# Heads 4 to 7 of the inverse's 64-level products go to the other 64 PSUM rows, alternating between two column halves of the array

## The chip, the cores and the metric

The kernel runs on one core of one Trainium2 chip. What counts is the device time of a run in microseconds; the median of several runs is given, and one execution was taken with the hardware profiler. Engines are named as in the profile: PE is TensorE's matmul, PEld its weight load, DVE is VectorE, ACT is ScalarE, POOL is GpSimd, SP is the queue from which most DMAs are issued.

## The reference

One layer with a bidirectional gated delta rule (8 heads of 128, two directions), a gated short convolution, a merge and a layer norm over 2048 latent and 256 context tokens. The part that matters here is the inverse of a unit lower triangular matrix in each chunk:

```
m = jnp.where(tri_strict, jnp.einsum('bhncd,bhnsd->bhncs', k_beta, k) * decay, 0.0)
eye = jnp.eye(CHUNK, dtype=jnp.float32)
t_inv = lax.linalg.triangular_solve(eye + m, jnp.broadcast_to(eye, m.shape), left_side=True, lower=True)
u = jnp.einsum('bhncs,bhnsv->bhncv', t_inv, v_beta)
w = jnp.einsum('bhncs,bhnsd->bhncd', t_inv, k_beta * jnp.exp(g_cum)[..., None])
...
def step(s, xs):
    v_new = u_i - jnp.einsum('bhck,bhkv->bhcv', w_i, s)
    o = jnp.einsum('bhck,bhkv->bhcv', q_dec_i, s) + jnp.einsum('bhcs,bhsv->bhcv', qk_i, v_new)
    s = s * d_i[..., None, None] + jnp.einsum('bhck,bhcv->bhkv', k_dec_i, v_new)
```

## The kernel before

The kernel has three stages: the input projections (to about 1890 us of the span), the window, in which the delta rule runs (about 1890 to 2865 us), and the dense tail.

The window makes 36 blocks: 18 chunks of 128 tokens, two directions, forward and backward in turn, so block 14 and every other even one goes forward. Blocks are counted here from 0, in the order of their 64-level products. The loop (`window`) is a pipeline over blocks: in one turn block k+2 gets its matrix N (`gram` "N" on L158 to L163, then `inv_base`), block k has the middle of its inverse done (`inv_w16` to `inv_d64`), and block k-1 is used (`st_ks`, `st_v`, `st_o`, `st_u`). From block 20 on the products behind N and QK were kept in DRAM by the other direction and are loaded (L151), so that those turns have no gram products.

Between these steps stand fillers: 24 to 27 dense 128x512 matmuls a turn (L1244, L1246, L1248, tile pf) of the output branches. PE's order is written out by hand. For the other engines a scheduler picks the order at build time, and each engine then runs its list strictly in that order.

The inverse of one block goes up in levels. The 16-level is done on DVE (L186 to L188, fifteen steps on the tile R16, shown as R and rb), and ACT copies its end into r32 (L191). Then come products on PE at 16, 32 and 64. A 64-level turn is, on PE: `inv_w64` (L273, eight heads, contracting over 64 rows, the result in 64 rows of a PSUM tile pinv), nine fillers, `inv_d64` (L283, again eight heads), the gram products of block k+2 (L158), nine fillers, `st_ks` of the next block (L295). ACT copies the first product into w64 (L276), and writes minus the second into R (L284), on which st_v then works.

A 64-level product before contracts over rows p1 (or p2) and leaves all eight heads in the same 64 PSUM rows, so all eight use the same quarter of the array, one after the other. Each fp32 matmul stands in the trace as two records.

What else the prediction speaks of: `visit_decay` (gcb: the DMA on L104, eight DVE steps L140, the ACT exponential L142, the DVE product L143, into which N and QK are then multiplied on L163); ACT copies gram's PSUM into zat (L161) before DVE reads it on L163; ACT takes four pieces of N (L172) and L175, and DVE goes on with L176; DVE's vh (L297) reads st_ks.

Of the kernel before, what the change touches and what calls it, by code (L numbers as in the profile page):

```python
# [18 lines left out]
H = 8  # L19
# [18 lines left out]
class Kern:  # L38
# [229 lines left out]
    def inv_w64(self, v):  # L268
        nc = self.nc
        (p1, p2), = self.blocks(v["d"], 64)  # L270
        wp = self.pi.tile([P, H, 64], F32, name="pinv")
        for h in range(H):
            nc.tensor.matmul(wp[p2, h, :], v["N"][p1, h, p2], v["r64t"][p1, h, :], start=True, stop=True)  # L273
        v["w64"] = self.g2.tile([P, H, 64], F32, name="w64", bufs=1)
        with self.tc.high_priority(100):
            nc.scalar.copy(out=v["w64"][p2], in_=wp[p2])  # L276

    def inv_d64(self, v):
        nc = self.nc
        (p1, p2), = self.blocks(v["d"], 64)  # L280
        dp = self.pi.tile([P, H, 64], F32, name="pinv")
        for h in range(H):
            nc.tensor.matmul(dp[p1, h, :], v["w64"][p2, h, :], v["r64"][p2, h, :], start=True, stop=True)  # L283
        nc.scalar.mul(out=v["R"][p1, :, p2], in_=dp[p1], mul=-1.0)  # L284


    def st_ks(self, v):
# [1353 lines left out]
```

## Time and profile before

| what | value |
|---|---|
| three runs | 3212.18, 3214.05, 3216.02 us; median 3214.05 us |
| the profiled execution | 3216.19 us |
| its span, first to last instruction | 3214.5 us |
| mean granted TensorE clock over the span | 0.965 |
| PE busy | 2939.6 us, 91% of the span |
| PEld busy | 2410.3 us, 75% |
| DVE busy | 2197.9 us, 68% |
| ACT busy | 1518.0 us, 47% |
| POOL busy | 1405.7 us, 44% |

Busy shares are averages over the three stages; only the window holds the changed products. A busy PE is not a PE at its peak, since a matmul's end is modelled.

### The profile page before, as it was taken

The page shows a single profiled execution, that of the slowest core. Times are in us where ns is not written, and L with a number is a line of the kernel's source. Part 1 is how long each engine was busy: PE and PEld are TensorE (multiplying, and loading weights), DVE is VectorE, ACT ScalarE, POOL GpSimd, SP SyncE. Part 2 cuts the span into 40 slices and gives each one's busy share as a digit, 9 for nine tenths or more (in the row PEclk, how much of TensorE's full clock was granted, in tenths as well). Part 3 has the DMA queues.
Part 4 walks back from the last instruction along what each step waited for, and adds up shares of the span by engine and source line. Part 5 has one row for each costly group of instructions (what it writes and reads, how often), then busy time and mean ns, then how long its engine had stood idle before and what let it go on. Part 6 is the DMA issues. An engine that isn't in the chain of part 4 may idle for free.

```text
span 3214.5 us, 60268 instructions
## 1 busy us (share of the span) xinstructions
PE 2939.6 (91%) x22089; PEld 2410.3 (75%) x22089; DVE 2197.9 (68%) x5663; ACT 1518.0 (47%) x3405; POOL 1405.7 (44%) x1016
## 2 busy tenths in 40 slices
PE   7899889999998999999999978999998888896897
PEld 4678668888887777788878767888887777784776
DVE  7756746566655575565552268888889999867399
ACT  4563553333345746333344335565655666653121
POOL 3543547766567555566666401111111132315264
PEclk9999999999999999999999989999999889998999
DMA  5533763323565433132243377676687777777742
GB/s 212 142 109 86 231 214 121 102 79 113 179 192 173 134 86 100 53 86 85 79 124 109 111 282 253 220 268 222 214 299 257 242 237 267 240 264 251 243 153 102
DMA packets 405381, 557.24 MB, mean 173 GB/s; under 512 B 28244, under 2 KB 278613, under 8 KB 404060
## 3 DMA queue, kind: packets, MB, share of 16 engines
q1 hardware_dynamic: 382158, 520.77, 51.0%
q10 hardware_dynamic: 22926, 32.62, 2.8%
q8 instruction: 173, 2.83, 0.4%
q14 instruction: 124, 1.02, 0.1%
HBM read 391.66 MB, written 161.64 MB: 172 GB/s over the span
## 4 chain that ended last, share of the span: by engine, by line
PE 43%; DVE 27%; DMA 8%; issue 7%; ACT 6%; POOL 5%; SPq 1%; ACTq 0%; DVEq 0%; POOLq 0%
PE pd L758 12%; PE pd L760 12%; PE pd L759 11%; DVE rb L187 3%; DMA gcb<-gcd 3%; POOL al L342 3%; DVE rb L186 2%; DVE gcb L140 2%; DVE R L188 2%; ACT n L172 1%; DVE t L1003 1%; POOL s L744 1%; DVE S L328 1%; DVE gcb L143 1%; DVE t L1005 1%
## 5 line engine op out<-in xcount | busy, mean ns | idle before, releaser
L758 PE MATMUL pd<-bh,ah 128*128 128x512 f32 x2240 | 891.3, 398 | 10.3 <-ACT u L778 5.8
L760 PE MATMUL pd<-bh,al 128*128 128x512 f32 x2240 | 878.7, 392 | 0.0
L759 PE MATMUL pd<-bl,ah 128*128 128x512 f32 x2240 | 878.2, 392 | 0.0
L342 POOL TENSOR_TENSOR al<-s,ah 128x512 fp32r<-128x512 f32 x348 | 478.4, 1378 | 471.2 <-ACT ah L341 466.2
L342 POOL TENSOR_TENSOR al<-raw,ah 128x512 fp32r<-128x512 f32 x260 | 371.9, 1435 | 323.6 <-ACT ah L341 288.9
L758 PEld LDWEIGHTS pd<-bh,ah 128*128 128x128 f32 x2240 | 424.6, 190 | 98.9 <-issue 6.6
L760 PEld LDWEIGHTS pd<-bh,al 128*128 128x128 f32 x2240 | 424.1, 189 | 90.7 <-POOL al L342 0.2
L759 PEld LDWEIGHTS pd<-bl,ah 128*128 128x128 f32 x2240 | 424.8, 190 | 85.9
L341 ACT CAST ah<-s 128x512 fp32r<-128x512 f32 x352 | 214.6, 618 | 298.5 <-PE pd L759 261.7
L341 ACT CAST ah<-raw 128x512 fp32r<-128x512 f32 x264 | 162.3, 616 | 257.8 <-PE pd L759 166.3
L744 DVE TENSOR_TENSOR s<-s,raw 128x512 f32<-128x512 f32 x80 | 107.0, 1338 | 220.7 <-POOL s L744 220.7
L1244 PE MATMUL pf<-ah,wh 128*128 128x512 f32 x512 | 212.4, 416 | 44.4 <-DMA wh<-w_ahd 17.7
L138 POOL TENSOR_TENSOR qd<-qd,qT 128x1024 f32<-128x1024 f32 x32 | 75.7, 2367 | 393.7 <-ACT qd L137 376.7
L1248 PE MATMUL pf<-ah,wl 128*128 128x512 f32 x512 | 218.4, 427 | 2.5 <-DMA wl<-w_ald 2.5
L1246 PE MATMUL pf<-al,wh 128*128 128x512 f32 x512 | 211.0, 412 | 0.7 <-POOL al L342 0.6
L187 DVE TENSOR_TENSOR rb<-rb,n 128x56 f32<-128x56 f32 (+5 forms) x540 | 171.6, 318 | 7.1
L1244 PEld LDWEIGHTS pf<-ah,wh 128*128 128x128 f32 x512 | 101.4, 198 | 66.5 <-issue 29.4
L188 DVE TENSOR_TENSOR R<-R,rb 128x56 f32<-128x56 f32 (+5 forms) x540 | 131.3, 243 | 5.5
L1020 ACT ACTIVATE t<-t 128x512 f32<-128x512 f32 (+1 forms) x112 | 67.2, 600 | 142.2 <-DVE t L1005 142.1
L118 POOL TENSOR_TENSOR kt<-kt,kd 128x1024 f32<-128x1024 f32 x36 | 73.0, 2029 | 137.5 <-DMA kt<-kd 130.8
L315 PE MATMUL pst<-S,qd 128*128 128x128 f32 x512 | 105.5, 288 | 20.3 <-ACT v L307 12.0
L1248 PEld LDWEIGHTS pf<-ah,wl 128*128 128x128 f32 x512 | 100.9, 197 | 26.8 <-DMA wl<-w_ald 6.1
(353 smaller groups left out, 5941.3 us busy)
## 6 DMA issues: line engine op xcount, KB each, us to landing
raw<-in_w_in SPq DMA_DIRECT2D x160, 512.0 KB
kT<-kTd SPq DMA_DIRECT2D x36, 512.0 KB
gcb<-gcd SPq DMA_DIRECT2D x36, 512.0 KB
kt<-kd SPq DMA_DIRECT2D x36, 512.0 KB
vh<-vd SPq DMA_DIRECT2D x36, 512.0 KB
wh<-w_bhd SPq DMA_DIRECT2D x32, 512.0 KB
wl<-w_bld SPq DMA_DIRECT2D x32, 512.0 KB
qT<-qTd SPq DMA_DIRECT2D x32, 512.0 KB
```

The source lines that it names most:

```text
L187: nc.vector.tensor_tensor(out=rbv, in0=rbv, in1=bc(n16[:, :, i:i + 1], w), op=ALU.mult)
L188: nc.vector.tensor_tensor(out=R[:, :, c0:c1], in0=R[:, :, c0:c1], in1=rbv, op=ALU.add)
L315: nc.tensor.matmul(po[:, j, :], v["qd"][:, h, :], S[:, h, :], start=True, stop=False)
L341: self.nc.scalar.copy(out=hi, in_=src)
L342: (eng or self.nc.gpsimd).tensor_tensor(out=lo, in0=src, in1=hi.bitcast(F32), op=ALU.subtract)
L744: eng.tensor_tensor(out=o, in0=a, in1=b, op=op)
L758: mm(ps, hi[:, k, :], bh, start=(first and k == 0), stop=False, skip_group_check=not first)
L759: mm(ps, hi[:, k, :], bl, start=False, stop=False, skip_group_check=not first)
L760: mm(ps, lo[:, k, :], bh, start=False, stop=(last and k == 3), skip_group_check=not first)
L1244: mm(ps, wh[:, k, :], ah, start=(k == 0), stop=False)
L1246: mm(ps, wh[:, k, :], al, start=False, stop=False)
L1248: mm(ps, wl[:, k, :], ah, start=False, stop=(k == KT - 1))
```

## The change

In both products the heads are taken in pairs, h and h + 4. Heads 0 to 3 write the PSUM rows that they wrote before, heads 4 to 7 the other 64 rows, which are the other 64 columns of the array; the rows of the array (the contraction) stay the same. What was one ACT instruction on 64 rows and eight heads becomes two on 64 rows and four heads each, in `inv_w64` and in `inv_d64`.

```diff
         wp = self.pi.tile([P, H, 64], F32, name="pinv")
-        for h in range(H):
+
+        for h in range(4):
             nc.tensor.matmul(wp[p2, h, :], v["N"][p1, h, p2], v["r64t"][p1, h, :], start=True, stop=True)
+            nc.tensor.matmul(wp[p1, h + 4, :], v["N"][p1, h + 4, p2], v["r64t"][p1, h + 4, :], start=True, stop=True)
         v["w64"] = self.g2.tile([P, H, 64], F32, name="w64", bufs=1)
         with self.tc.high_priority(100):
-            nc.scalar.copy(out=v["w64"][p2], in_=wp[p2])
+            nc.scalar.copy(out=v["w64"][p2, 0:4], in_=wp[p2, 0:4])
+            nc.scalar.copy(out=v["w64"][p2, 4:8], in_=wp[p1, 4:8])
...
         dp = self.pi.tile([P, H, 64], F32, name="pinv")
-        for h in range(H):
+        for h in range(4):
             nc.tensor.matmul(dp[p1, h, :], v["w64"][p2, h, :], v["r64"][p2, h, :], start=True, stop=True)
-        nc.scalar.mul(out=v["R"][p1, :, p2], in_=dp[p1], mul=-1.0)
+            nc.tensor.matmul(dp[p2, h + 4, :], v["w64"][p2, h + 4, :], v["r64"][p2, h + 4, :], start=True, stop=True)
+        nc.scalar.mul(out=v["R"][p1, 0:4, p2], in_=dp[p1, 0:4], mul=-1.0)
+        nc.scalar.mul(out=v["R"][p1, 4:8, p2], in_=dp[p2, 4:8], mul=-1.0)
```

The scheduler lays out ACT, DVE, POOL and SP anew, since the number of ACT instructions changed. In the changed kernel the lines behind the edit stand five lower (L158 and L142 are unmoved, L1248 is L1253); the new ones are L274 and L275 for the first product, L278 and L279 for its copies, L286 and L287 for the second product, L288 and L289 for its results.

ACT's list in block 14, before, from the end of the 32-level to the first gram copy:

```order
L260 ACTIVATE r_21466<-pinv 32x8x32
L262 ACTIVATE r64t<-pinv 32x8x32 [waits PE_49]
L266 ACTIVATE R<-r_21466,m64l 128x8x64 [waits Activation_49]
L276 COPY w_21621<-pinv 64x512 [waits PE_49]
L266 ACTIVATE R<-r_21466,m64h 128x8x64
L191 ACTIVATE r_21334<-R_21286,m16l 128x8x16 [waits DVE_49]
L191 ACTIVATE r_21334<-R_21286,m16h 128x8x16
L142 ACTIVATE gcb<-gcb 128x1024
L284 ACTIVATE R<-pinv 64x8x64 [waits PE_49,Activation_49]
L161 COPY zat<-gram 128x512 [waits PE_49]
```

The same place of the changed kernel (r_21362 is block 15's r32, of which R_21314 is the 16-level result on DVE):

```order
L262 ACTIVATE r64t<-pinv 32x8x32 [waits PE_49]
L266 ACTIVATE R<-r_21494,m64l 128x8x64 [waits Activation_49]
L266 ACTIVATE R<-r_21494,m64h 128x8x64
L278 COPY w_21649<-pinv 64x256 [waits PE_49]
L142 ACTIVATE gcb<-gcb 128x1024 [waits DVE_49]
L191 ACTIVATE r_21362<-R_21314,m16l 128x8x16 [waits DVE_49]
L191 ACTIVATE r_21362<-R_21314,m16h 128x8x16
L279 COPY w_21649<-pinv 64x256
L288 ACTIVATE R<-pinv 64x4x64 [waits PE_49,Activation_49]
L289 ACTIVATE R<-pinv 64x4x64
L161 COPY zat<-gram 128x512 [waits PE_49]
```

The one copy of w64 stood ahead of L191 and L142; now its second half stands behind them. So it is in blocks 6, 8, 10, 12, 14, 16, 18 and 26 (L142, then L191 twice, in between), in block 19 (L191 twice, then L142) and in block 4 (L191 twice alone); in block 20 both halves stand behind L191 twice and L142. In the other 25 blocks the two halves follow each other directly, and in the odd blocks 5 to 17 they stand ahead of L191 as the one copy did.

PE's list at the second product of block 14 in the changed kernel, the last filler ahead of it and the gram products behind it (before, the eight L283 had one wait, on the first of them):

```order
L1251 MATMUL pf<-al_15726,wh 128x512
L286 MATMUL pinv<-r_21494,w_21649 64x64 [waits Activation_49]
L287 MATMUL pinv<-r_21494,w_21649 64x64 [waits Activation_49]
L286 MATMUL pinv<-r_21494,w_21649 64x64
L287 MATMUL pinv<-r_21494,w_21649 64x64
...
L158 MATMUL gram<-kT 128x128 [waits DMAHW6_49]
L158 MATMUL gram<-kT 128x128 x7
```

PE's order of steps is the same; the second matmul of the product now waits for the second copy by itself.

## Rows read from the trace of the kernel before

**Rows 1.** The page's first lines: span, and busy time of each engine.
```profile
span 3214.5 us, 60268 instructions
PE 2939.6 (91%) x22089; PEld 2410.3 (75%) x22089; DVE 2197.9 (68%) x5663; ACT 1518.0 (47%) x3405; POOL 1405.7 (44%) x1016
```
**Rows 2.** By stretch: us, then PE, PEld, DVE, ACT, POOL busy; clock, DMA share, GB/s.
```profile
2266.00:2319.20 53.20, 49.79 (x754) 43.76 (x753) 47.04 (x196) 31.88 (x66) 9.00 (x6) 1.00 0.68 219
...
2400.00:2860.00 460.00, 399.36 (x5785) 344.35 (x5784) 415.48 (x1707) 285.77 (x789) 114.85 (x74) 0.93 0.76 255
```
**Rows 3.** Chain that ended last, 2266 to 2296 us, by line.
```profile
by line: DMA gcb<-gcd 29.3%; DVE rb L187 21.4%; DVE rb L186 9.9%; DVE S L328 9.2%; DVE gcb L143 7.9%; DVE R L188 7.5%; DVE gcb L140 5.8%; ACT n L172 5.6%; issue 5.1%; DVE vh L297 5.0%; DVE QK L163 3.8%; DVE N L163 2.3%; DVE gt L1187 2.0%; A
```
**Rows 4.** What DVE waited for, 2000 to 2372 us: total, times, longest.
```profile
DVE n L176 <- ACT n L175: 21.8, 13, 1.7
DVE t L128 <- DMA gcb<-gcd: 12.5, 13, 3.9
```
**Rows 5.** What PE waited for, 1900 to 2860 us: total, times, longest.
```profile
PE pst L295 <- DVE ot L1285: 16.5, 10, 2.8
...
PE pinv L256 <- ACT w32i L245: 8.7, 10, 4.5
PE pinv L205 <- DVE R L188: 8.5, 2, 4.3
```
**Rows 6.** PE in order of time around block 14: start, length, instruction.
```profile
2270.70 1.14 PE L273 MATMUL pinv<-r64t,N 64*64 64x64 f32 x16 [0.39 <-ACT r64t L262]
...
2274.03 1.14 PE L283 MATMUL pinv<-r,w 64*64 64x64 f32 x16
2275.11 2.05 PE L158 MATMUL gram<-kT 128*128 128x128 f32 x16
...
2279.06 2.07 PE L295 MATMUL pst<-S,kT 128*128 128x128 f32 x16
```
**Rows 7.** Chain that ended last: the first and last of its fourteen 64-level products.
```profile
1904.72 1.32 PE pinv L273 x16
...
2860.46 1.09 PE pinv L283 x16
```
**Rows 8.** Busy time of instructions on pinv in two stretches, as in rows 2.
```profile
2743.00:2743.90 0.90, 0.86 (x14) 0.86 (x15) 0.00 (x0) 0.00 (x0) 1.00 0.95 332
2294.40:2294.95 0.55, 0.54 (x48) 0.54 (x48) 0.00 (x0) 0.00 (x0) 1.00 0.90 335
```
**Rows 9.** ACT in order of time around block 14.
```profile
2269.87 0.38 ACT L260 ACTIVATE r<-pinv 32x256 f32<-32x256 f32 x1
...
2271.88 0.58 ACT L276 COPY w<-pinv 64x512 f32<-64x512 f32 x1 [0.48 <-PE pinv L273]
...
2275.62 0.40 ACT L191 ACTIVATE r<-R,m16l 128x128 f32<-128x128 f32 x1 [2.41 <-DVE R L188]
...
2276.22 1.04 ACT L142 ACTIVATE gcb<-gcb 128x1024 f32<-128x1024 f32 x1
2277.29 0.59 ACT L284 ACTIVATE R<-pinv 64x512 f32<-64x512 f32 x1
```
**Rows 10.** DVE in order of time around block 14.
```profile
2275.30 0.28 DVE L188 TENSOR_TENSOR R<-R,rb 128x120 f32<-128x120 f32 x1
...
2277.30 2.37 DVE L143 TENSOR_TENSOR gcb<-gcb,cc 128x1024 f32<-128x1024 f32 x1
...
2280.53 0.67 DVE L163 TENSOR_TENSOR N<-gram,gcb 128x512 f32<-128x512 f32 x1
2281.13 0.59 DVE L297 SCALAR_TENSOR_TENSOR vh<-pst,ngam,vh 128x128 f32<-128x128 f32 x2
2283.39 0.35 DVE L176 SCALAR_TENSOR_TENSOR n<-n,m16h,n 128x128 f32<-128x128 f32 x1 [1.68 <-ACT n L175]
```
**Rows 11.** The 3.5 us behind two of the long waits of rows 5.
```profile
1973.28:1976.78 3.50, 3.50 (x56) 3.15 (x57) 2.01 (x8) 3.29 (x6) 0.00 (x0) 0.50 0.49 152
...
2669.71:2673.21 3.50, 3.50 (x70) 2.95 (x71) 3.50 (x21) 0.37 (x1) 0.00 (x0) 0.50 0.99 319
```

## The prediction

> **What bounds the kernel now.** I read the page first: PE is busy 91% of the span of 3214.5 us, DVE 68% [rows 1]. Those are averages over three stages, and the 72 changed products lie in the window alone, so next I took stretches of it. Two turns there, 53.2 us, hold 49.79 us of PE and 47.04 of DVE at a clock of 1.00; over the later 460 us PE is busy 399.36 and DVE 415.48, with the clock at 0.93 [rows 2]. Both engines are nearly full, so shares don't say which sets the pace. The chain does. Over 30 us around blocks 14 and 15 it consists of DVE's base steps (L186 to L188), gcb and S steps, the DMA of gcb and ACT's pieces of N (L172), with no PE step among the lines shown [rows 3]. What the reader is to see is a closed loop: the second half of N (L163), ACT, L176, the base steps, QK, then gcb's buffer free, its DMA, the decay, the next N. DVE's own waits fit: 21.8 us in 13 waits for ACT's L175 and 12.5 in 13 for the DMA of gcb [rows 4]; PE is not among them. So in blocks 5 to 17 PE has a little slack, and a shorter product mostly makes it wait longer for DVE. Where PE does wait long in the window, it is for DVE or ACT [rows 5].
>
> **The products.** In block 14 the second product starts at 2274.03 and the gram products behind it at 2275.11: 1.08 us for 16 records, 67 ns each [rows 6]. The new pairs share the array's rows and differ in its columns. The trace of before has such a pair at 32 wide: L256 and L258 contract over the same 32 rows and write different ones. With L257 in a third place they make 48 records in 0.54 us, 34 ns for one of each; fourteen records of the 64-wide kind on one place fill 0.86 [rows 8]. If L256 and L258 took turns, a triple would need twice the time of one record, so they run side by side. Eight records to a half at 67 ns then give 0.54 us, and a product saves 0.54. The bounds are 0 (the halves take turns) and 0.54; I take 0.5. All 72 would be 36 us of PE time, but only fourteen products stand on the chain, at the window's two ends and scattered over its second half [rows 7]: 14 x 0.5 = **-7 us**. The rest is covered by DVE's loop.
>
> A rule speaks against this part: the Trainium skill, page "TensorE: Matmul & The Clock Gate", Part 3 on packing small matmuls, The mechanism, says that a weight load overlaps matmuls in flight only where its row group differs. By it the new pairs would gain nothing. L256 and L258 overlap in spite of it [rows 8], so I keep 0.54, and the rule's case is a rival below.
>
> **The copies.** One copy of 64x512 takes 0.58 us and L284 0.59; the nearest row for 256 columns is L260, 0.38 [rows 9]. Two for one cost 0.17 more. In the odd blocks with gram products L284 stands between L142, on which DVE's gcb hangs, and the gram copies that N needs, so there it is on the path: seven blocks by 0.17, **+1 us** (bounds 0 and 2). Elsewhere ACT's gaps hide it (the wait of 2.41 us ahead of L191 in rows 9); without that cover it would be 72 x 0.17 = 12 us.
>
> **What the new order moves.** This is the largest term. In block 14 the copy was done at 2272.46, ahead of L191 and L142 [rows 9]. Now its second half stands behind both, and L191 needs the end of DVE's base, which comes at 2275.30 + 0.28 = 2275.6 [rows 10]. From there L142 takes 1.04, the two L191 0.6 (2275.62 to 2276.22), the copy 0.38 [rows 9]: done at 2277.6. PE comes to the second product at 2274.03 less the 0.5 of the first [rows 6], issues head 0, and waits at head 4 for **about 4 us**. Behind it in PE's order are the gram products for N, nine fillers and st_ks.
>
> At full clock the rest of the product takes 0.5 and gram 1.8 (2275.11 to the next filler, nine fillers of 2.15 us ahead of 2279.06) [rows 6], so gram ends near 2280.0. With 0.6 us for its ACT copy, the second N starts at 2280.6, where it started at 2280.53 [rows 10]: the wait goes into slack that PE had against DVE. st_ks then gives its first four heads at 2280.0 + 2.15 + 0.9 = 2283.1, and DVE's two vh end at 2283.7, 0.3 later than L176 could start, 2283.39 [rows 10]. So +0.3 us is the lower bound for a block.
>
> But the clock does not stay. The trace has waits of PE of up to 4.5 and 4.3 us [rows 5], and in the 3.5 us behind two of them the granted clock is 0.50, the lower of its two levels, 1.2 GHz [rows 11]. The new wait is as long. At half speed the 2.3 us of product and gram become 4.2 or so; N is 2.0 to 2.2 late, and with vh **+2.5 us** is the upper bound. I take 2.0, nearer to the upper end because rows 11 are the nearest case. DVE being the loop, it makes up nothing of it. Six blocks have this order and gram products behind it (6, 8, 10, 12, 14, 16): **+12 us**, bounds 2 and 15. In block 4 the base was done long ahead, and I count nothing.
>
> In blocks 18, 19, 20 and 26 the copy is late as well, but N is loaded, so only st_ks is behind it, ahead of which PE waited anyway: 16.5 us in ten waits for ot [rows 5]. The excess of a 3 to 4 us wait over 1.65 passes on in part: 1 us each, **+4 us**, bounds 0 and 9.
>
> **Sum.** -7 + 1 + 12 + 4 = +10 us. The profiled execution took 3216.2 us, 1.7 more than its span and 2.1 more than the median of the three runs, so +10 gives 3226.2 for such an execution and **3224 us** on the medians. No load or store is added; the DMA queues only get a new order.
>
> **Rivals.**
> *Full clock.* If the clock holds through the 4 us waits, or the waits come out shorter, the six blocks cost 2 and the four others 1: -7 + 1 + 2 + 1 = -3, 3211 us. For it: some waits of 2 to 3 us in the second half cost little. Against it: rows 11.
> *TensorE sets the pace* (the faster one). PE's busy share is above DVE's in the first half [rows 2]. If in truth DVE comes to N, vh and S just when PE lets it, each turn of the 31 from block 5 on returns up to 1 us, and a good half of that, -20 net of the late copies, gives 3194. It decides if DVE's idle time in a turn ends on PE more often than on ACT or the DMA; rows 3 and 4 speak against it.
> *The halves take turns.* Then the products still need 1.08 us, the first term is gone, and the rest stays: +17, 3231 us. Its point is whether 16 records take 1.08 or 0.54. Rows 8 speak against it, the rule cited above for it.
>
> **Chances and range.** Forecast 0.50, full clock 0.22, TensorE's pace 0.18, halves in turn 0.10. A difference of 0.2%, 6.4 us, is about what a measurement of this kernel can tell from no change. Slower by more: most of the forecast's 0.50 and the 0.10, 0.55. Within it: the full clock and the forecast's lower edge, 0.27. Faster: 0.18. With all late-copy costs at their upper bounds and the products' gain, -7 + 2 + 15 + 9 = +19, and without that gain +26, 3240; at the lower bounds -7 + 0 + 2 + 0 = -5, 3209. The range is 3207 to 3240 us; it leaves out most of TensorE's pace. The forecast's own range is 3216 to 3233.
>
> **What would show it.** The sixteen records of a product in 0.5 to 0.6 us, not 1.08, show the first term; L278 and L279 at 0.36 to 0.40 the second. PE waiting 3 to 4 us for L279 in blocks 6, 8, ..., 18, then a clock of 0.50 and a second N (L163) about 2 us later against the base's end, show the third; two turns of that stretch should take 55 and not 53.2 us. It is wrong if those two turns take 53 or less (the waits are absorbed), if the clock stays at 1.00, or if the odd blocks get shorter by what PE saves.

## The result and the profile after

The changed kernel took 3249.18 us (median; 3244.53 to 3254.31), the kernel before, run beside it, 3215.0 us. The ratio is 1.0108, with a 95% interval of 1.0088 to 1.0129: slower by 34 us. Its four executions took 3244.5, 3245.4, 3253.0 and 3254.3 us, so the median is good to a few us only; the profiled one is the shortest, with a span of 3242.8. The first lines of its page, which answer to [rows 1]:

```profile
span 3242.8 us, 60334 instructions
PE 2929.7 (90%) x22089; PEld 2395.6 (74%) x22089; DVE 2213.9 (68%) x5663; ACT 1526.8 (47%) x3477; POOL 1409.9 (43%) x1016
```

TensorE is busy 10 us less and the span is 28 us longer. ACT's 72 more instructions are its split copies. PE in order of time around block 14, against [rows 6] (start, length, instruction, and in brackets how long the engine stood idle and for whom):

```profile
2281.04 0.27 PE L274 MATMUL pinv<-r64t,N 64*64 64x64 f32 x1 [0.38 <-ACT r64t L262]
2281.05 0.27 PE L275 MATMUL pinv<-r64t,N 64*64 64x64 f32 x1
...
2281.51 0.22 PE L275 MATMUL pinv<-r64t,N 64*64 64x64 f32 x1
2281.65 0.50 PE L1253 MATMUL pf<-ah,wl 128*128 128x512 f32 x1
...
2287.86 0.36 PE L287 MATMUL pinv<-r,w 64*64 64x64 f32 x1 [3.61 <-ACT w L279]
...
2288.89 3.78 PE L158 MATMUL gram<-kT 128*128 128x128 f32 x16
2292.33 0.77 PE L1253 MATMUL pf<-ah,wl 128*128 128x512 f32 x1
```

The two matmuls of a pair start 10 ns apart, and the next instruction comes 0.61 us after the first (2281.65 - 2281.04), where it was 1.08 [rows 6]. So the pairs do run side by side. Then the second product stands 3.61 us for the second copy, and the gram products behind it need 3.44 us to the next filler (2292.33 - 2288.89), where they needed 1.8, as the next filler in the trace of before shows (2276.91 - 2275.11 in [rows 6]):

```profile
2276.91 0.47 PE L1248 MATMUL pf<-ah,wl 128*128 128x512 f32 x1
```

ACT around block 14 of the changed kernel, against [rows 9]:

```profile
2282.38 0.37 ACT L278 COPY w<-pinv 64x256 f32<-64x256 f32 x1
2285.77 1.06 ACT L142 ACTIVATE gcb<-gcb 128x1024 f32<-128x1024 f32 x1 [3.03 <-DVE gcb L140]
2286.74 0.39 ACT L191 ACTIVATE r<-R,m16l 128x128 f32<-128x128 f32 x1
2287.03 0.38 ACT L191 ACTIVATE r<-R,m16h 128x128 f32<-128x128 f32 x1
2287.44 0.36 ACT L279 COPY w<-pinv 64x256 f32<-64x256 f32 x1
2289.06 0.38 ACT L288 ACTIVATE R<-pinv 64x256 f32<-64x256 f32 x1 [1.26 <-PE pinv L287]
2289.45 0.38 ACT L289 ACTIVATE R<-pinv 64x256 f32<-64x256 f32 x1
...
2292.71 0.58 ACT L161 COPY zat<-gram 128x512 f32<-128x512 f32 x1 [1.01 <-PE gram L158]
```

The first half is copied at 2282.38. The other half has been ready almost as long, but ACT stands 3.03 us at L142, does the two L191, and copies it at 2287.44. DVE, against [rows 10], and what the late N leads to:

```profile
2285.66 0.27 DVE L188 TENSOR_TENSOR R<-R,rb 128x120 f32<-128x120 f32 x1
...
2293.33 0.69 DVE L163 TENSOR_TENSOR N<-gram,gcb 128x512 f32<-128x512 f32 x1 [1.02 <-ACT zat L161]
2295.93 0.61 DVE L302 SCALAR_TENSOR_TENSOR vh<-pst,ngam,vh 128x128 f32<-128x128 f32 x2 [1.91 <-PE pst L300]
2296.46 0.34 DVE L176 SCALAR_TENSOR_TENSOR n<-n,m16h,n 128x128 f32<-128x128 f32 x1
...
2307.01 0.17 DVE L128 SCALAR_TENSOR_TENSOR t<-gc,gcb 128x8 f32<-128x8 f32 x1 [1.51 <-DMA gcb<-gcd]
```

From the end of the base (2285.66 + 0.27 = 2285.93) the second N starts 7.40 us later; it was 4.95 [rows 10]: 2.45 late. L176 is 2.7 late, the second QK 3.0, and L128, which waits for the next gcb, 3.9. So there is a second loss behind the one that the prediction saw. SyncE's queue shows where:

```profile
2299.52 0.32 SPq L109 DMA_DIRECT2D qT<-qTd  x1
2301.65 0.32 SPq L104 DMA_DIRECT2D gcb<-gcd  x1
```

and the chain of waits has the length of that load:

```profile
2301.65 5.33 DMA gcb<-gcd
```

Here the load of gcb starts 2.13 us after that of qT and takes 5.33 us. In the trace of before the distance at this place is 4.41 us and the load takes 4.44:

```profile
2283.86 0.32 SPq L109 DMA_DIRECT2D qT<-qTd  x1
2288.27 0.32 SPq L104 DMA_DIRECT2D gcb<-gcd  x1
```

```profile
2288.27 4.44 DMA gcb<-gcd
```

How much of the loss arises where can be summed from such rows over blocks 6, 8, 10, 12, 14 and 16, the changed kernel against before, each step counted from the end of the base: the second N is 10.4 us late (block 10 not at all, the others 1.3 to 2.5), the second QK 14.3, L128 22.1, and the next base ends 22.1 late. More than half of the loss in these blocks arises behind the second N.

Stretches of the changed kernel, columns as in [rows 2]: two turns, cut at the same place in a turn as in [rows 2], a stretch that begins within the wait, and the later 460 us:

```profile
2276.34:2333.62 57.28, 50.07 (x755) 44.40 (x754) 46.24 (x196) 32.48 (x70) 9.56 (x6) 0.94 0.62 206
2286.25:2293.07 6.82, 5.21 (x32) 5.00 (x33) 3.56 (x10) 3.34 (x9) 2.65 (x2) 0.50 0.35 114
2400.00:2860.00 460.00, 385.26 (x5612) 328.99 (x5611) 422.73 (x1705) 280.10 (x788) 114.76 (x73) 0.89 0.74 248
```

From 2286.25 us, while PE still waits, the granted clock is 0.50 for 6.8 us. It falls to 0.50 at the waits of blocks 6, 8, 12, 14 and 16, and once for some 3 us at 2252; in the trace of before it stays at 1.00 from 1998 to 2386 us. All in all, PE waited for L279 this much between 2000 and 2390 us:

```profile
PE pinv L287 <- ACT w L279: 20.6, 6, 3.6
```

### The profile page after: what moved, and what is told of

Same layout as the page of the kernel before. It is cut to its first block, busy times and chain, and to the rows that moved or that the text cites. A ratio compares the mean times of both kernels' runs of the same rounds, so it can differ in the third digit from the quotient of the medians.

```text
span 3242.8 us, 60334 instructions
## 1 busy us (share of the span) xinstructions
PE 2929.7 (90%) x22089; PEld 2395.6 (74%) x22089; DVE 2213.9 (68%) x5663; ACT 1526.8 (47%) x3477; POOL 1409.9 (43%) x1016
## 4 chain that ended last, share of the span: by engine, by line
PE 45%; DVE 25%; DMA 8%; issue 7%; ACT 6%; POOL 5%; SPq 1%; ACTq 0%; DVEq 0%; POOLq 0%
PE pd L763 12%; PE pd L764 12%; PE pd L765 12%; DMA gcb<-gcd 3%; DVE rb L187 3%; POOL al L347 3%; DVE gcb L140 3%; DVE R L188 2%; DVE rb L186 2%; POOL s L749 1%; DVE t L1008 1%; PE gram L158 1%; ACT n L172 1%; PE pd L1097 1%; DVE t L1010 1%
## 5 line engine op out<-in xcount | busy, mean ns | idle before, releaser
L1253 PE MATMUL pf<-ah,wl 128*128 128x512 f32 x512 | 223.2, 437 | 3.5 <-DMA wl<-w_ald 3.4
L187 DVE TENSOR_TENSOR rb<-rb,n 128x56 f32<-128x56 f32 (+5 forms) x540 | 161.1, 298 | 7.1
L188 DVE TENSOR_TENSOR R<-R,rb 128x56 f32<-128x56 f32 (+5 forms) x540 | 138.1, 256 | 5.9
L140 DVE SCALAR_TENSOR_TENSOR gcb<-gcb,gc,mask 128x128 f32<-128x128 f32 x288 | 127.0, 448 | 3.1 <-ACT qd L137 1.9
L1253 PEld LDWEIGHTS pf<-ah,wl 128*128 128x128 f32 x512 | 103.8, 203 | 29.0 <-DMA wl<-w_ald 7.6
```

The lines of the kernel that those rows point to most:

```text
L140: nc.vector.scalar_tensor_tensor(out=gcb[:, h, :], in0=gcb[:, h, :], scalar=gcT[:, h:h + 1], in1=self.mask[d], op0=ALU.subtract, op1=ALU.min)
L187: nc.vector.tensor_tensor(out=rbv, in0=rbv, in1=bc(n16[:, :, i:i + 1], w), op=ALU.mult)
L188: nc.vector.tensor_tensor(out=R[:, :, c0:c1], in0=R[:, :, c0:c1], in1=rbv, op=ALU.add)
L1253: mm(ps, wl[:, k, :], ah, start=False, stop=(k == KT - 1))
```

## The experiments

The theory at this point: the late second copy is the whole loss. The rivals: the halves themselves, the longer list of ACT instructions, or a wait elsewhere. A kernel in which only the copies' place differs tells most.

**e1, copies early.** The place of the copies in ACT's order comes from a priority:

```diff
-        with self.tc.high_priority(100):
+        with self.tc.high_priority(400):
             nc.scalar.copy(out=v["w64"][p2, 0:4], in_=wp[p2, 0:4])
             nc.scalar.copy(out=v["w64"][p2, 4:8], in_=wp[p1, 4:8])
```

> The changed kernel with one edit: the priority of the two w64 copies is 400 and not 100, which puts both halves ahead of L191 and L142 on ACT in every block; PE's list is the same. If the late second copy is the cost, PE no longer waits for it, the clock holds through blocks 6 to 18, and what is left is the shorter products on the chain (-7) and the extra ACT time (+1): 3209 us, between 3203 and 3216. If the halves themselves or the 72 more ACT instructions slow the kernel, it stays near 3249 us.

Measured: 3217.51 us against 3217.12, ratio 1.0006 (0.9996 to 1.0016). The loss is gone with the place of the copies. But nothing is gained: the 7 us for shorter products don't come, and the time lies above the range that was expected of this kernel. PE of this kernel at block 14 shows where they go there:

```profile
2278.43 1.05 PE L300 MATMUL pst<-S,kT 128*128 128x128 f32 x8
2280.27 1.16 PE L300 MATMUL pst<-S,kT 128*128 128x128 f32 x8 [0.79 <-DVE S L333]
```

In the kernel before, the sixteen records of this line ran through without a wait [rows 6]. What TensorE saves in two products it now stands idle for DVE's S; the second N starts 4.94 us after the base, as before.

**e2, split copies alone.** The kernel before, products untouched, copies split by heads:

```diff
-            nc.scalar.copy(out=v["w64"][p2], in_=wp[p2])
+            nc.scalar.copy(out=v["w64"][p2, 0:4], in_=wp[p2, 0:4])
+            nc.scalar.copy(out=v["w64"][p2, 4:8], in_=wp[p2, 4:8])
...
-        nc.scalar.mul(out=v["R"][p1, :, p2], in_=dp[p1], mul=-1.0)
+        nc.scalar.mul(out=v["R"][p1, 0:4, p2], in_=dp[p1, 0:4], mul=-1.0)
+        nc.scalar.mul(out=v["R"][p1, 4:8, p2], in_=dp[p1, 4:8], mul=-1.0)
```

> The kernel before with its two ACT instructions per block cut into two of four heads each, products unchanged on PE. In this build both copies stand ahead of L191 and L142 in all blocks but 19. If the place of the copy is the cost, this takes +1 for the extra ACT time and +1 for block 19: 3217 us, between 3214 and 3221. If 72 more ACT instructions are the cost, most of the 34 us, 3240 or more.

Measured: 3217.09 us, ratio 0.9994 (0.9981 to 1.0007). 72 more ACT instructions cost nothing that can be measured.

**e3, second product alone.** The changed kernel with `inv_w64` as before:

```diff
-        for h in range(4):
-            nc.tensor.matmul(wp[p2, h, :], ...)
-            nc.tensor.matmul(wp[p1, h + 4, :], ...)
+        for h in range(H):
+            nc.tensor.matmul(wp[p2, h, :], ...)
...
-            nc.scalar.copy(out=v["w64"][p2, 0:4], in_=wp[p2, 0:4])
-            nc.scalar.copy(out=v["w64"][p2, 4:8], in_=wp[p1, 4:8])
+            nc.scalar.copy(out=v["w64"][p2], in_=wp[p2])
```

> The changed kernel with inv_w64 as it was before: the first product and its single copy as before, only the second product in column halves with its two results. The one copy stands ahead of L191 and L142 in every block. Late-copy theory: half of the products' gain on the chain, -3, and +1 for L288 and L289: 3213 us, between 3208 and 3217. If working in column halves costs by itself, about half of 34 us: 3232.

Measured: 3220.43 us, ratio 1.0018 (1.0008 to 1.0028). No gain either, in 36 products that are each half a microsecond shorter; if anything it is 0.2% slower, above the range expected.

**e4, work in the wait.** The changed kernel, late copies kept; useless matmuls are added ahead of the second product of six blocks (`k` is the block's number):

```diff
         dp = self.pi.tile([P, H, 64], F32, name="pinv")
+        if v["k"] in (6, 8, 10, 12, 14, 16):
+            for _ in range(4):
+                nc.tensor.matmul(dp, self.ident, v["kT"][:, 0:4, :], start=True, stop=True)
```

> The changed kernel, copies as late as there, with four 128x512 fp32 matmuls (about 0.86 us each at full clock, 3.4 together) of no use written into the second product's PSUM tile ahead of it in blocks 6, 8, 10, 12, 14 and 16. PE reaches the second product as late as before, about when the copy is done, but has not been idle. If the fall of the clock behind the wait is most of the price, the granted clock stays at 1.00 there, the second N comes about 0.3 us and not 2.45 us later against the base's end, and some 2.5 to 3 us a block come back: 3232 us, between 3228 and 3237. If the wait itself is the price and the clock adds little, it stays at 3245 to 3253.

Measured: 3241.18 us, ratio 1.0083 (1.007 to 1.0097), between the two ranges. In the trace the clock stays at 1.00 behind the waits of blocks 6, 8, 12, 14 and 16, and these five cost 1.2 to 2.2 us each in place of 3.5 to 5.6 (from the end of the base to the next first product, against before). Block 10 got 5.3 us in place of 1.6: ahead of it TensorE had stood 2.2 us for S and its fillers ran at 0.50, so that the second copy was done at 2176.18, before the added matmuls began at 2176.25. There was no wait left to fill, and they came on top. So one block spoiled the comparison, but the clock is not all of the price. The next kernels leave block 10 out.

**e5, late in five.** Late copies in five blocks alone:

```diff
-        with self.tc.high_priority(100):
+        with self.tc.high_priority(100 if v["k"] in (6, 8, 12, 14, 16) else 400):
```

> The changed kernel with both halves of w copied ahead of the waiting ACT instructions in every block except 6, 8, 12, 14 and 16, where the second half stays behind L191 as in the changed kernel. Theory (a late copy costs 3.9 us a block: the second N comes 2.45 us later, and the load of gcb that follows falls together with the load of qT and the stores of kqd and takes 1 to 2 us longer): the sum over these five blocks was 21 us in the trace of the changed kernel, so 3217 + 21 = 3238 us (3233 to 3243). Rival (the price that the prediction took, 2.0 us a block, and the rest of the loss elsewhere): 3217 + 10 = 3227 us. Rival (the copy costs only with its neighbours in blocks 18, 19 and 26 late too): about 3220 us.

Measured: 3240.77 us against 3217.91, ratio 1.0074 (1.0057 to 1.009): 23 us more than e1, 4.7 a block.

**e6, work in five waits.** The kernel of e5 with the four matmuls of e4 in the same five blocks.

> The kernel of e5 with four useless matmuls of 128x512 into dp ahead of the second product in the same five blocks, so that TensorE does not stand still while the late copy is awaited; nothing is left out. Theory (the granted clock at 0.50 after the wait is about half of the price, the other half is the load of gcb that meets the load of qT and the kqd stores): in the trace of e4 these five blocks were 1.2 to 2.2 us longer than before, 9 us together, so 3217 + 9 = 3226 us (3222 to 3231). Rival (the clock plays no part, the wait itself is the price): 3238 us as e5. Rival (the clock is the whole price): 3217 us.

Measured: 3227.35 us, ratio 1.0024 (1.0013 to 1.0036). PE at block 14, where the first row is the four matmuls, in eight records:

```profile
2272.97 3.60 PE L287 MATMUL pinv<-kT,ident 128*128 128x512 f32 x8
...
2276.99 0.27 PE L290 MATMUL pinv<-r,w 64*64 64x64 f32 x1 [0.18 <-ACT w L279]
...
2277.60 2.05 PE L158 MATMUL gram<-kT 128*128 128x128 f32 x16
```

The stretch from 0.3 us behind the base's end on, as the one of the changed kernel above:

```profile
2275.40:2282.20 6.80, 6.62 (x50) 5.15 (x49) 4.24 (x11) 4.25 (x11) 2.66 (x2) 1.00 0.40 150
```

The copy is as late as in e5, but the clock stays at 1.00 and gram takes 2.05 us in place of 3.78. The second N is 0.73 us late in place of 2.45. That gives back 13.4 of the 23 us, 2.7 a block.

**e7, early in six.** Priority 400 in blocks 6, 8, 10, 12, 14, 16 and 100 in the others, the reverse of e5 but for block 10.

> The changed kernel with both halves copied early in blocks 6, 8, 10, 12, 14 and 16 alone; blocks 4, 18, 19, 20 and 26 keep the late second half. Theory (the six even blocks carry 23 of the 32 us, the later ones the rest): 3217 + 7 = 3224 us (3219 to 3229). Rival (the six are all of it): 3217 us. Rival (the price lies in the later blocks): 3235 us or more.

Measured: 3223.34 us, ratio 1.0023 (1.0012 to 1.0035): the late copies of blocks 4, 18, 19, 20 and 26 cost 6 us over e1.

**e8, third gcb.** The kernel before with `self.pool(es, "gb", 3)` in place of 2.

> The kernel before with three buffers for gcb in place of two, nothing else changed: its load no longer waits until the tile of the turn before is free. Theory (that load's 4.2 to 4.8 us lie on the chain of waits in every block of the first half, 17 per cent of the chain between 2040 and 2400 us, and VectorE's L128 waits 13.4 us for it): the load moves away from the chain and what was behind it comes earlier, 0.5 to 2 us in each of some 25 blocks: 3195 us (3170 to 3212). Rival (the base of the inverse on VectorE or the kqd store is next in line, and takes the place of the load): 3217 us.

Measured: 3218.92 us, ratio 1.0008 (0.9994 to 1.0022): no gain. In its trace the load at block 14 still starts when the second QK has been read (2287.11 us), now for the visit after the next, and DVE's L128 of that later visit stands earlier in its order and still waits for it (1.52 us at that place). Why the order came out so stays open.

**e9 to e11, qT early.** To set the load of gcb apart from that of qT, qT got two buffers: in e5 (e9), in e6 (e10), and in e1 as control (e11).

```diff
-            v["qT"] = self.g1.tile([P, H, P], F32, name="qT")
+            v["qT"] = self.g1.tile([P, H, P], F32, name="qT", bufs=2)
```

> The kernel of e5 with two buffers for qT in place of one, so that its load is issued a gram earlier, right behind that of kT, and is over when the load of gcb begins; late copies in the same five blocks. Theory (of the 4 us of a late block 1.0 to 1.5 are the load of gcb that meets the load of qT): 3240.8 - 5 x 1.2 = 3235 us (3230 to 3238). Rival (the load of gcb is long for the kqd stores alone, or the lag comes from elsewhere): 3241 us as e5.

> The kernel of e6 (late copies in five blocks, four useless matmuls in each wait) with two buffers for qT. Theory: what was left in e6 over the kernel with early copies, 10 us, is five times 0.74 us of a later second N and five times 1.2 us of the load of gcb; the second part goes: 3217 + 4 = 3221 us (3217 to 3225). Rival (the load of qT plays no part): 3227 us as e6.

> The kernel of e1 (products in halves, all copies early) with two buffers for qT: the control for e9 and e10. Without a late copy the load of qT is issued 4.4 us ahead of that of gcb already. Theory: 3217 us as e1 (3213 to 3220). Rival (the load of qT lies on the path in every block): 3210 us or less.

Measured, against 3214.67: e9 3242.54 us, ratio 1.009 (1.007 to 1.0111); e10 3230.76, 1.0046 (1.003 to 1.0063); e11 3226.97, 1.0042 (1.0028 to 1.0055). The edit did not do what it was meant to, as SyncE's queue in e9 shows:

```profile
2300.56 0.32 SPq L109 DMA_DIRECT2D qT<-qTd  x1
2302.69 0.32 SPq L104 DMA_DIRECT2D gcb<-gcd  x1
```

The two loads are 2.13 us apart as ever in a late block. The control lost 10 us against e1 by something else, which stays open. The three runs decide nothing about the load.

**e12, first product alone.** The first product and its two copies as changed, the second product (`inv_d64`) as before.

> The first product in halves with its two copies, the second as in the kernel before. ACT's order then has the second copy behind L191 in blocks 6, 8, 12, 14, 16 and 19, and between L142 and L191 in 10 and 18. Theory (the late copy is the whole cost, whoever the reader): 3217 + 21 and 1 to 5 more for block 19 and the others: 3240 us (3235 to 3247). Rival (the cost needs the second product's two passes): 3220 us, as the second product alone had.

Measured: 3238.93 us against 3214.67, ratio 1.0077 (1.0056 to 1.0098). The loss comes with the second copy of w, whatever form the reader has.

**e13 to e15, five loads of qT left out.** In e1 (e13, the control), e5 (e14) and e6 (e15), the five visits whose qT is loaded right after the late blocks take the tile of the visit before:

```diff
         if v["latent"]:
-            v["qT"] = self.g1.tile([P, H, P], F32, name="qT")
+            if v["k"] in (9, 11, 15, 17, 19):
+                v["qT"] = self.qT
+                return
+            v["qT"] = self.qT = self.g1.tile([P, H, P], F32, name="qT")
```

> Products in halves and all copies early, as e1; the visits 9, 11, 15, 17 and 19 read the qT of the visit before, so that five loads of qT (512 KB each) are left out. It is the control for the next two. Expected 3217 us (3212 to 3220): with early copies the load of gcb starts 4.4 us after that of qT and took 4.2 to 4.5 us with it, so that taking qT away changes nothing there.

> The kernel of e5 (late copies in blocks 6, 8, 12, 14, 16) without the five loads of qT that follow these blocks, by the same edit. Theory (in a late block the load of gcb starts only 2.1 us after that of qT, shares the queues with it, and takes 5.0 to 6.0 us in place of 4.4): the gcb loads come back to about 4.4 us, 1.2 us x 5 = 6 us, so 3235 us (3231 to 3238). Rival (the two kqd stores, 1.4 and 2.4 us ahead, are what makes it long): gcb stays above 5 us and the time at 3241 us.

> The kernel of e6 (late copies in five blocks, four useless matmuls in each wait) without the same five loads of qT. Theory: of the 10 us that e6 was above the kernel with early copies 6 go, and 5 x 0.74 us of a later second N stay: 3221 us (3217 to 3224). Rival (the stores of kqd): 3227 us as e6.

Measured, against 3217.72: e13 3216.25 us, ratio 0.9993 (0.9984 to 1.0002); e14 3229.93, 1.0039 (1.0028 to 1.005); e15 3218.3, 1.0004 (0.9991 to 1.0018). In the chain of e14 the load after block 14 now reads:

```profile
2298.03 4.20 DMA gcb<-gcd
```

and in that of e15:

```profile
2292.76 4.51 DMA gcb<-gcd
```

The stores of kqd are still there, about as far ahead as in e5 and e6, and so is the load of kT, so it was the load of qT that made it long. In the control nothing changes by leaving it out. Of the ten loads of gcb in the late blocks of e14 and e15 nine took 4.2 to 4.5 us; one, behind block 12 of e14, still took 5.58. e14 gained more than was expected (3231 to 3238), e15 came out as expected.

Block 14 in these kernels, in us from the end of the base to the start of each step, worked out from the rows:

| kernel | second N | second QK | L128 (gcb is there) | next first product |
|---|---|---|---|---|
| before | 4.95 | 11.97 | 17.16 | 21.71 |
| changed | 7.40 | 15.01 | 21.08 | 25.63 |
| e6, clock held | 5.68 | 12.72 | 19.16 | 23.72 |
| e14 (e5, no qT load) | 7.40 | 15.31 | 20.24 | 25.19 |
| e15, both | 5.69 | 12.74 | 17.99 | 22.54 |

## Why the prediction was right in its direction and wrong in its size

*The products.* That the pairs overlap was right: 0.61 us for sixteen records, near the 0.54 forecast. The Trainium skill, page "TensorE: Matmul & The Clock Gate", Part 3, The mechanism, has a weight load overlap matmuls in flight only where the row group differs. The two halves of a pair share their rows, so by that sentence alone the product would still need some 1.08 us; the measured 0.61 decides against it here. The rival in which the halves take turns falls with it. But the term's size, -7 us, was wrong: e1 has the shorter products without late copies and gains nothing, nor does e3. The chain of before ran through fourteen products [rows 7], and that a step is on the chain does not say by how much the next one would follow a shorter step. In block 14 a wait for DVE's S takes 0.8 us. That block is not one of the fourteen, and for those the cause was not shown; near the window's start the trace of e1 is 0.8 us ahead of before at the first product of block 1 (1929.85 against 1930.66) and level at block 3 (1977.28 in both).

*The copies.* L278 and L279 take 0.37 and 0.36 us, L288 and L289 0.38, as estimated from [rows 9]. The term of +1 us is not to be seen in e2; it lies within what can be measured.

*The late copy in six blocks.* This is the step that failed. **The term was +12 us, with +15 as its bound; it is about 26 by the medians** (3249.2 less the 3217.5 of e1 is 32, and e7 gives 6 of it to the other blocks) **and 22 in the profiled execution.** The mechanism as far as it went is in the trace: PE waits 3.6 us for L279 ("about 4 us"), the clock goes to 0.50, and the second N comes late by 10.4 us in six blocks, where 12 was taken for all of it. Block 10, with a wait of 2.5 us and no fall of the clock, has no late N. What failed is what was put behind N: next to nothing.

Above all, the load of gcb, which the prediction left out by closing its count at L176. "The DMA queues only get a new order" was the sentence that passed over it. The load starts when QK has been read, and in a late block all of that is squeezed together: it starts 2.13 us after the load of qT, not 4.41 us after, and takes 5.0 to 6.4 us, not 4.2 to 4.8. Its cost by e14 against e5, with the control's 1.3 us taken off, is 9.6 us, 1.9 a block; by e15 against e6 it is 7.8, 1.6 a block. In the profiled executions of e6 and e15 the five blocks differ by 1.1 us each on average, and the rows of the load itself by 1.0 to 1.2; the intervals of the runs are several us wide, so 1.1 to 1.9 is as near as it is known.

Beside it, the clock. The wait was reckoned to cost 0.3 us a block at full clock and 2.5 at half, and 2.0 was taken. The first is near what was measured: e15 lies 2 us above e13 with five late copies, 0.4 a block, though their intervals overlap; their profiled executions differ by 0.8 a block. The clock was to add 2.2 between the bounds. It adds 2.7 a block by e5 against e6 and 2.3 by e14 against e15, where no load of qT is in the way; in the profiled executions 2.1 and 2.2. So the clock was sized about right between the bounds, and the 2.0 taken was somewhat low. Added step by step, the wait (e13 to e15), the load (e15 to e6) and the clock (e6 to e5) cost 0.4, 1.6 and 2.7 us a block by the medians and 0.8, 1.1 and 2.1 in the profiled executions. That is 4.7 and 4.0 a block, where 2.0 was taken.

*The other late blocks.* +4 us, with bounds of 0 and 9, was taken for blocks 18, 19, 20 and 26; e7 measures 6.

*The rivals.* "Full clock" falls by the trace; its reasoning, that the wait alone is nearly absorbed, is what e15 shows (0.4 to 0.8 us a block). "TensorE sets the pace" falls by e1: with 24 us less of TensorE's work the time is the same. Two turns took 57.3 us; 55 was forecast, and 53.2 was measured before [rows 2].

## What to carry to other kernels

When one copy becomes two, look where the scheduler puts the second: behind an in-order engine's wait it makes the reader as late as that wait, and a place in the order, not the work, decided 32 us here. Carry such a delay through the whole loop, past the first step that is late, to the loads that its end releases: a load that is issued later may meet another one. And shortening a step that the chain passes through pays only if what is next is not waiting for another engine already.

## What was not expected of the hardware

A 512 KB load (gcb) that starts 2.1 to 2.3 us behind another of 512 KB (qT) took 4.9 to 6.4 us in the late blocks of the changed kernel and of e4 to e6, and 5.65 at the one such place in the trace of before (block 4). 4.0 to 4.8 us behind it, or without it, most took 4.2 to 4.8, while the two kqd stores of 256 KB 1.4 and 2.4 us ahead made no such difference (e14, e15). Not all loads fit: among others two in the trace of before, at blocks 9 and 17, took 8.9 and 7.0 us at 4.0 and 4.7 us behind that of qT, and why stays open. And eight records (four matmuls of 128x512) in a 3.6 us wait, doing nothing useful, kept the granted clock at 1.00 in each of the five waits (e6), and that alone made a kernel 13 us shorter.
